# A hybrid decoder on one core: all K pairs of a fast quarter by Winograd, some of their factors made ahead

## The chip, the cores and the metric

The kernel runs on one core of a Trainium2 chip. The time is that of the device in microseconds, from the first to the last instruction and what lies around it; a comparison is between the kernel before and the kernel after on the same chip. The matmul engine is TensorE (PE in the profile), the others are VectorE (DVE), ScalarE (ACT), GpSimd (POOL) and SyncE (SP), which here only issues transfers.

## The reference

Two layers over 256 positions of width 2048, float32 throughout. Each sub-layer is `x <- LN(alpha*x + f(x))` with `alpha = 4 ** 0.25`:

```python
# layer 0: gated convolution, then MLP
bcu = x @ w_in                       # 2048 x 6144
gate_b, gate_c, u = split(bcu, 3)
y = causal_depthwise_conv(gate_c * u, conv_w, width=3)
x = LN(alpha * x + (gate_b * y) @ w_out)
x = LN(alpha * x + square(relu(x @ w1[0])) @ w2[0])     # 2048 -> 8192 -> 2048
# keys and values from a latent of 512, 16 heads, rotary part of 64
# layer 1: latent attention, then MLP
x = LN(alpha * x + attention(x) @ w_o)
x = LN(alpha * x + square(relu(x @ w1[1])) @ w2[1])
```

## The kernel before

**Products.** A float32 operand is split in a high part, which TensorE multiplies at full speed, and the low rest. `split` (L125 to L128) does it: ScalarE casts (L127), VectorE subtracts (L128). A product of 128 output columns is 16 K tiles of a matmul of 512 columns (`high`, L215: high weights by high and low activations side by side) and one of 256 (`low`, L219: low weights by high activations). The down projections use `dot` (L300, L302, L303), three matmuls of 512 columns: high by high, low weights, low activations.

**The stream of weights.** All weights lie in one list, `stream`, in the order of their use. `take` hands the next entry to TensorE's code and first begins the preparations of the entries up to `LOOK = 5` steps ahead. A plain tile of 1024 columns is one step: a load of 512 KB on SP's queue in a pool of raw tiles (`RAW` of them) and a split into a pool of high and low tiles (`WA` of them). A fast pair is three steps, below. The instruction order in each engine's queue comes from a scheduler; each engine then runs its queue in order.

**The MLP.** The hidden width of 8192 is worked in eight quarters `q` (the kernel's word; a quarter is 1024 columns, eight chunks of 128). A quarter has a product part (eight products, each evacuated, Relu and Square taken, split) and a down part, which adds the quarter's share to the output, 256 by 2048. Quarters 1 to 6 are fast (`FAST`): the output is four column blocks of 512 in two groups `g` of two, the positions are two halves of 128, and a pair of K tiles times a pair of column blocks is done by the Winograd form of Strassen's scheme: seven `dot`s (`FACTORS`: the sums "3", "1", "5", "7", "2", "6", "4") in place of eight. It needs derived factors on both sides. On the weight side `prepare` makes T1 and T3 (L162, 1024 columns), T2 (L166) and T4 (L169, 512 columns each) on VectorE from the pair's two raw tiles and splits all: three splits of 1024 and one of 512. On the side of the hidden activations `form` makes S1 to S4 from two chunks (L707 to L710, four VectorE instructions of 128 columns) and splits them.

The seven sums of a group are more than the eight PSUM banks allow for both groups at once. So a group's sums are copied into PSUM (ScalarE, L612), all pairs are added by TensorE, and the sums copied out (ScalarE, L616), or, where a sum began from zero, added to its place by VectorE (L624). Four of the seven are sums that go to several output blocks and are held in `sums`, the others go to the block they belong to (`acc`); `fold` spreads the held ones in quarter 7. In group 1 only three of the four pairs were fast (`MIXED = "sssp"`); the plain pair's 24 matmuls include one that is done as two halves of 256 (`EVEN`). Group 0 had four fast pairs.

**Around it.** `Norm` works on the residual `xres` (16 chunks), and its `prepare` ran for the residual of MLP0 in quarter 7. In MLP1 `turn_residual` transposes the residual and adds it to `acc` (L1027, L1028), two of eight in each of quarters 1 to 4. In attention the output product's chunks (`out_first`) are interleaved with the stages of the last heads (`together`, with the counts `BEHIND`).

## Time and profile before

| | us |
|---|---|
| median of three runs | 1998.59 (1996.66 to 1999.63) |
| profiled execution, first to last instruction | 1994.9 |
| TensorE busy in it | 1987.7 |
| VectorE busy | 1709.4 |
| ScalarE busy | 1354.9 |
| product part of a fast quarter (536.00 to 580.40) | 44.40 |
| down part of it (580.40 to 619.23) | 38.83 |

The profile has no total of its own for its execution, only the span; the median of the runs is 3.7 us longer than that span. In the profile's rows an L number is a line of the kernel. A group's row reads: line, engine, operation, output and inputs by the program's names, their shapes, the count, then busy time and the mean of one in ns, then the idle time of the engine just before them and what ended it. A timeline row reads: start, length, engine, line, operation, with the idle time before it in brackets. A windows row gives the length of a stretch and each engine's busy time and count in it, then the granted clock, the share of the DMA engines and their GB/s.

### The profile page before, as it was taken

The page shows a single profiled execution, that of the slowest core. Times are in us where ns is not written, and L with a number is a line of the kernel's source. Part 1 is how long each engine was busy: PE and PEld are TensorE (multiplying, and loading weights), DVE is VectorE, ACT ScalarE, POOL GpSimd, SP SyncE. Part 2 cuts the span into 40 slices and gives each one's busy share as a digit, 9 for nine tenths or more (in the row PEclk, how much of TensorE's full clock was granted, in tenths as well). Part 3 has the DMA queues.
Part 4 walks back from the last instruction along what each step waited for, and adds up shares of the span by engine and source line. Part 5 has one row for each costly group of instructions (what it writes and reads, how often), then busy time and mean ns, then how long its engine had stood idle before and what let it go on. Part 6 is the DMA issues. An engine that isn't in the chain of part 4 may idle for free.

```text
span 1994.9 us, 30180 instructions
## 1 busy us (share of the span) xinstructions
PE 1987.7 (100%) x11110; PEld 1737.2 (87%) x11110; DVE 1709.4 (86%) x2555; ACT 1354.9 (68%) x2154; POOL 2.3 (0%) x21
## 2 busy tenths in 40 slices
PE   9999999999999999999999999999999999999998
PEld 8888888988888888888889998898888888888886
DVE  8667667797999989989978988777899999999985
ACT  6444445586778778777756755558677787887772
POOL 0000000000000000000000000000000000000000
PEclk9999999999999999999999999999999999999999
DMA  8666666565657466574855543656464656656483
GB/s 318 205 191 187 190 190 190 179 193 157 212 170 251 148 216 221 177 243 147 281 171 159 170 140 123 201 180 195 146 233 155 232 161 220 222 178 233 150 269 130
DMA packets 106853, 385.85 MB, mean 193 GB/s; under 512 B 11857, under 2 KB 12625, under 8 KB 106449
## 3 DMA queue, kind: packets, MB, share of 16 engines
q1 hardware_dynamic: 106560, 383.79, 59.5%
q8 instruction: 87, 1.43, 0.3%
q14 instruction: 62, 0.50, 0.1%
q10 hardware_dynamic: 144, 0.13, 0.0%
HBM read 381.78 MB, written 2.10 MB: 192 GB/s over the span
## 4 chain that ended last, share of the span: by engine, by line
PE 98%; DVE 1%; ACT 1%; issue 0%; DVEq 0%; ACTq 0%
PE ps_u L215 20%; PE ps_l L215 13%; PE ps_u L219 10%; PE ps_l L219 7%; PE ps_f L300 4%; PE ps_f L303 4%; PE ps_f L302 4%; PE ps_r L303 4%; PE ps_r L302 4%; PE ps_r L300 4%; PE ps_d L300 2%; PE ps_d L302 2%; PE ps_d L303 2%; PE ps_w L249 2%; PE ps_w L248 2%; PE ps_w L247 2%
## 5 line engine op out<-in xcount | busy, mean ns | idle before, releaser
L128 DVE TENSOR_TENSOR lo<-raw,hi 128x1024 fp32r<-128x1024 f32 x710 | 861.8, 1220 | 190.6 <-ACT hi L127 119.9
L127 ACT CAST hi<-raw 128x1024 fp32r<-128x1024 f32 x710 | 741.8, 1051 | 247.4 <-PE ps_l L215 98.1
L215 PE MATMUL ps_u<-xhl,hi 128*128 128x512 f32 x1792 | 621.7, 392 | 0.0
L219 PE MATMUL ps_u<-xhl,lo 128*128 128x256 f32 x1792 | 498.2, 279 | 0.0
L215 PEld LDWEIGHTS ps_u<-xhl,hi 128*128 128x128 f32 x1792 | 334.5, 187 | 73.6 <-ACT acc L595 0.2
L219 PEld LDWEIGHTS ps_u<-xhl,lo 128*128 128x128 f32 x1792 | 338.1, 189 | 1.8
L215 PE MATMUL ps_l<-xhl_a,hi 128*128 128x512 f32 x704 | 244.1, 393 | 0.0
L219 PE MATMUL ps_l<-xhl_a,lo 128*128 128x256 f32 x704 | 195.4, 279 | 0.0
L215 PEld LDWEIGHTS ps_l<-xhl_a,hi 128*128 128x128 f32 x704 | 132.1, 188 | 29.9
L219 PEld LDWEIGHTS ps_l<-xhl_a,lo 128*128 128x128 f32 x704 | 131.9, 188 | 0.2
L127 ACT CAST hi_t<-raw_t 128x1024 fp32r<-128x1024 f32 x84 | 88.5, 1054 | 45.8 <-DVE raw_t L162 41.4
L162 DVE TENSOR_TENSOR raw_t<-raw,raw 128x1024 f32<-128x1024 f32 x84 | 102.3, 1218 | 1.8 <-DMA raw<-in_w2f_dram 1.5
L128 DVE TENSOR_TENSOR lo_t<-raw_t,hi_t 128x1024 fp32r<-128x1024 f32 x84 | 102.4, 1219 | 0.2
L718 ACT ACTIVATE fp<-fp 128x256 f32<-128x256 f32 x96 | 40.0, 416 | 63.2 <-DVE fp L356 62.6
L215 PE MATMUL ps_l<-z,hi 128*128 128x512 f32 x240 | 82.4, 391 | 0.0
L300 PE MATMUL ps_d<-hi,h 128*128 128x512 f32 x192 | 75.0, 391 | 0.0
L302 PE MATMUL ps_d<-lo,h 128*128 128x512 f32 x192 | 75.0, 390 | 0.0
L303 PE MATMUL ps_d<-hi,h 128*128 128x512 f32 x192 | 74.8, 389 | 0.0
L249 PE MATMUL ps_w<-xd,hi 128*128 128x258 f32 x256 | 72.7, 284 | 0.0
L248 PE MATMUL ps_w<-xd,lo 128*128 128x258 f32 x256 | 72.3, 282 | 0.0
L247 PE MATMUL ps_w<-xd,hi 128*128 128x258 f32 x256 | 72.3, 282 | 0.0
L215 PE MATMUL ps_l<-oT,hi 128*128 128x512 f32 x208 | 71.3, 391 | 0.0
(296 smaller groups left out, 3963.7 us busy)
## 6 DMA issues: line engine op xcount, KB each, us to landing
raw<-in_w_dram SPq DMA_DIRECT2D x344, 512.0 KB, 4.5
raw<-in_w2f_dram SPq DMA_DIRECT2D x168, 512.0 KB, 3.9
raw<-in_w_in_dram SPq DMA_DIRECT2D x88, 512.0 KB, 4.2
raw<-in_w_out_dram SPq DMA_DIRECT2D x32, 512.0 KB, 3.7
raw<-in_w_o_dram SPq DMA_DIRECT2D x32, 512.0 KB, 4.2
raw<-in_w_kv_dram SPq DMA_DIRECT2D x10, 512.0 KB, 3.7
raw<-in_w_q_dram SPq DMA_DIRECT2D x8, 512.0 KB, 4.0
raw<-in_w_uk_dram SPq DMA_DIRECT2D x8, 512.0 KB, 3.9
```

Source lines behind the costliest of these rows:

```text
L127: nc.scalar.copy(hi, src)
L128: nc.vector.tensor_tensor(lo, src, hi.bitcast(F32), ALU.subtract)
L162: nc.vector.tensor_tensor(t.rearrange(two, a=2), b12.unsqueeze(1).to_broadcast([P, 2, BW]), r1.rearrange(two, a=2), ALU.subtract)
L215: nc.tensor.matmul(ps, w[blk // 8][0][:, blk % 8, :], x, start=first, stop=False)
L219: nc.tensor.matmul(ps[:, :T], w[blk // 8][1][:, blk % 8, :], x[:, :T], start=False, stop=last)
L247: nc.tensor.matmul(ps[:, :W], hi, x[k][:, :W], start=k == 0, stop=False)
L248: nc.tensor.matmul(ps[:, :W], lo, x[k][:, :W], start=False, stop=False)
L249: nc.tensor.matmul(ps[:, :W], hi, x[k][:, W:], start=False, stop=k == NC - 1)
L300: nc.tensor.matmul(ps, x[0], w[0], start=first, stop=False, skip_group_check=onto)
L302: nc.tensor.matmul(ps[:, at], x[0], w[1][:, at], start=False, stop=False, skip_group_check=onto)
L303: nc.tensor.matmul(ps, x[1], w[0], start=False, stop=last, skip_group_check=onto)
L718: nc.scalar.activation(f, f, AF.Relu)
```

## The change

- Group 1 has four fast pairs too; `MIXED` and `EVEN` go. All eight pairs of a fast quarter now take 7 `dot`s.
- For some pairs the derived factors are made ahead and stored in DRAM: two of eight pairs in each fast quarter of layer 0, one of eight in layer 1 (`EARLY`), eighteen in all. `making` loads the pair's two raw tiles on POOL's queue, makes the three differences on VectorE and stores two tiles of 512 KB on POOL's queue. One step of it is taken in each chunk of the convolution from the seventh on, in every third chunk where the output product is added, and for layer 1 in every second stage of the last heads. `issue_after` ties these to instructions already in POOL's and VectorE's queues. For such a pair `prepare` has four loads and only splits.
- The order of groups alternates by quarter (`groups`), and four sums of the second group stay in PSUM into the next quarter (`stay`). Sums are kept and the next begun one at a time as each ends (`turn`, `end`). The sums "3" and "1" (`FRESH`) always begin from zero and are added to their place by VectorE; the others are copied in and out by ScalarE.
- `hidden` puts the two chunks of a pair into one tile, takes Relu and Square over both at once, and `form` makes the four sums with three instructions and splits seven blocks of 128 in one of 896.
- In MLP0 the residual is written to DRAM in quarter 1, after its `Norm.prepare`, and loaded back in quarter 7 (`parked`, `xback`); `sums` takes its place. In MLP1 all eight `turn_residual` run in quarter 1. The order of `fold` is adapted.
- `RAW` goes from 5 to 7 and `WA` from 8 to 9.

```diff
-RAW, WA = 5, 8
+RAW, WA = 7, 9
...
-MIXED = "sssp"
-EVEN = (QC - 1, "22")
+EARLY = {0: ((1, 0), (1, 2)), 1: ((1, 1),)}
+FRESH = ("3","1")
...
+MAKE_FROM = 6
...
+    held_x = [xres]
+    parked = ctx.enter_context(tc.tile_pool(name="parked", bufs=1, space=bass.MemoryType.DRAM)).tile(
+        [P, NC, T], F32, tag="parked", name="parked")
...
+    def groups(q):
+        return (1, 0) if (q - FAST[0]) % 2 == 0 else (0, 1)
...
+    stored = ctx.enter_context(tc.tile_pool(name="stored", bufs=1, space=bass.MemoryType.DRAM))
+    made = {}
+    for l, q in [(l, q) for l in EARLY for q in FAST]:
+        for i, j in EARLY[l]:
+            t = stored.tile([2, P, 1024], F32, tag=f"m{l}_{q}_{i}_{j}", name=f"made{l}_{q}_{i}_{j}")
+            made[l, q, i, j] = (t[0], t[1])
...
-            for j, kind in enumerate(MIXED):
-                out += [(w2f[l, q, 1, j, 0], w2f[l, q, 1, j, 1])] if kind == "s" else \
-                    halves(w2[l, q, 2, j]) + halves(w2[l, q, 3, j])
-            out += [(w2f[l, q, 0, j, 0], w2f[l, q, 0, j, 1]) for j in range(QC // 2)]
+            for i, g in enumerate(groups(q)):
+                for j in range(QC // 2):
+                    out.append((w2f[l, q, g, j, 0], w2f[l, q, g, j, 1]) + made.get((l, q, i, j), ()))
...
+    def making(l):
+        for (k, q, i, j), (to13, to24) in made.items():
+            if k != l:
+                continue
+            name = f"{l}_{q}_{i}_{j}"
+            r1, r2, t = (raws.tile([P, 1024], F32, tag="raw", name=f"{g}{name}") for g in ("m1", "m2", "m3"))
+            with tc.issue_after(state["pool"].ins):
+                for r, src in zip((r1, r2), w2f[l, q, groups(q)[i], j]):
+                    nc.gpsimd.dma_start(r, src)
+            yield
+            b22, (b21, b12) = r1[:, BW:], (r2[:, :BW], r2[:, BW:])
+            two = "p (a c) -> p a c"
+            with tc.issue_after(state["dve"].ins):
+                nc.vector.tensor_tensor(t.rearrange(two, a=2), b12.unsqueeze(1).to_broadcast([P, 2, BW]),
+                                        r1.rearrange(two, a=2), ALU.subtract)
+                nc.vector.tensor_tensor(r1[:, :BW], b22, t[:, :BW], ALU.subtract)
+                nc.vector.tensor_tensor(r1[:, BW:], b21, r1[:, :BW], ALU.subtract)
+            nc.gpsimd.dma_start(to13, t)
+            state["pool"] = nc.gpsimd.dma_start(to24, r1)
...
+        def fourth(src):
+            f = state["fast"].tile([P, 2, BW], F32R, tag="t4", name=f"t4_{i}", bufs=2)
+            split(f[:, 0, :], f[:, 1, :], src)
+            return [f[:, 0, :], f[:, 1, :]]
...
+        if len(stream[i]) == 4:
+            r1, t13 = load_raw(f"{i}_0", stream[i][0]), load_raw(f"{i}_1", stream[i][2])
+            finished(r1, f"{i}_1")
+            yield
+            t24 = load_raw(f"{i}_2", stream[i][3])
+            b21 = raws.tile([P, 1024], F32, tag="raw", name=f"raw{i}_3")[:, :BW]
+            nc.sync.dma_start(b21, stream[i][1][:, :BW])
+            finished(t13, f"{i}_t")
+            yield
+            finished(t24, f"{i}_2")
+            ready[i] = {**named((("11", "22"), ("T1", "T3"), ("T2", "T4"))), "21": fourth(b21)}
+            yield
+            return
+        r1, r2 = (load_raw(f"{i}_{j}", src) for j, src in enumerate(stream[i]))
...
-    def fast_products(ps, x, forms, j, fresh, ready, onto=()):
+    LEFT = ("11", "22", "12", "S1", "S3", "S2", "S4")
+    def fast_products(ps, x, j, fresh, ready, onto=(), then=None):
         b, = take(1)
-        a = {"11": held(x[2 * j], 0), "12": held(x[2 * j + 1], 0), "22": held(x[2 * j + 1], 1)}
-        for i in range(4):
-            a[f"S{i + 1}"] = [forms[:, j, o, i * P:(i + 1) * P] for o in range(2)]
+        a = {n: [x[j // 2][:, j % 2, o, i * P:(i + 1) * P] for o in range(2)] for i, n in enumerate(LEFT)}
         for p, l, r in FACTORS:
             dot(ps[p], b[r], a[l], p in fresh, p in ready, onto=p in onto)
+            if then:
+                then(p)
...
+    def summed(ln, pss, add, m0=0, maker=iter(())):
         for m, ps in enumerate(pss, m0):
+            if m % 3 == 0:
+                next(maker, None)
             add(ps, m)
             ln.count(m)
...
+        if m >= MAKE_FROM:
+            next(before_mlp, None)
...
+        def first_sums(ps, banks, m):
+            g = groups(q)[0]
+            for p in {3: ("3", "1", "5", "7") if q == FAST[0] else (), 4: "2", 5: "6", 6: "4"}.get(m, ()):
+                banks.setdefault(p, busy[m % 4])
+                ps[p] = begun_sum(p, g, f"ps_r{p}", banks[p])
...
+        def new_sum(p):
+            return p in FRESH or (q == FAST[0] and p in OWN)
...
+        def keep(p, g, ps, since):
...
             at = place(p, g)
-            if q == FAST[0] and p in OWN:
+            if p not in FRESH or (since == FAST[0] and p in OWN):
                 nc.scalar.copy(at, ps)
             else:
                 nc.vector.tensor_tensor(at, at, ps, ALU.add)
...
+        def down_pairs(h, ps, banks, spare):
...
+            order = [p for p, _, _ in FACTORS]
+            stay = order[:4] if q < FAST[-1] else []
+            new = {p for p in order if new_sum(p)}
+            after, place_of = {}, {}
+            def begin_next(p, bank):
+                after[p], place_of[p] = begun_sum(p, second, f"ps_f{p}", bank), bank
+            def turn(p):
+                keep(p, first, ps[p], max(q - 1, FAST[0]) if p in order[:4] else q)
+                i = order.index(p) + 1
+                if i < len(order):
+                    begin_next(order[i], banks[p])
+            def end(p):
+                if p not in stay:
+                    keep(p, second, after[p], q)
+            held_on = set(order[:4]) if q > FAST[0] else set()
             for j in range(n):
-                fast_products(then, h, forms, j, set(then) - onto if j == 0 else (), then if j == n - 1 else (), onto)
-            for p, _, _ in FACTORS:
-                (put_back if p in onto or p in new else keep)(p, 0, then[p])
-            return (b3, b1, b5, b7), (b6, b2, b4, b22)
+                if j == n - 1:
+                    begin_next(order[0], spare)
+                fast_products(ps, h, j, new - held_on if j == 0 else (), ps if j == n - 1 else (),
+                              set(ps) - (new - held_on), turn if j == n - 1 else None)
+            for j in range(n):
+                fast_products(after, h, j, new if j == 0 else (), after if j == n - 1 else (),
+                              set(order) - new, end if j == n - 1 else None)
+            if stay:
+                return [banks[order[-1]]] + [place_of[p] for p in order[4:]], {p: after[p] for p in stay}, \
+                    {p: place_of[p] for p in stay}
+            return [banks[order[-1]]] + [place_of[p] for p in order[:3]], {}, {p: place_of[p] for p in order[3:]}
...
+            def form(j, u):
+                a21, a11, a12, s1, s2, s4 = (u[:, i * P:(i + 1) * P] for i in (0, 1, 3, 4, 6, 7))
+                two = u.rearrange("p (i c) -> p i c", c=P)
+                nc.vector.tensor_tensor(s1, a21, u[:, 2 * P:3 * P], ALU.add)
+                nc.vector.tensor_tensor(two[:, 5:7, :], two[:, 0:5:4, :], a11.unsqueeze(1).to_broadcast([P, 2, P]),
+                                        ALU.subtract)
                 nc.vector.tensor_tensor(s4, a12, s2, ALU.subtract)
-                split(forms[:, j, 0, :], forms[:, j, 1, :], sf.rearrange("p i c -> p (i c)"))
+                f = factors[j // 2][:, j % 2]
...
+                if q in FAST:
+                    if m % 2 == 0:
+                        pair.append(fast.tile([P, 8 * P], F32, tag="fp", name="fp"))
+                    u = pair[-1]
+                    evac(ps, u[:, (m % 2) * T:(m % 2 + 1) * T])
+                    if m % 2:
+                        for function in (AF.Relu, AF.Square):
+                            nc.scalar.activation(u[:, :2 * T], u[:, :2 * T], function)
+                        form(m // 2, u)
+                    return
...
-                    if extra and m == 0 and q <= NB:
+                    if extra and q == FAST[0] and m < NB:
                         for t in range(2):
-                            extra(block, q - 1, t, busy[2 + t])
+                            extra(block, m, t, busy[2 + t])
+                    if begin and q == FAST[0]:
+                        begin(range(max(2 * m, 1), 2 * m + 2))
+                        nc.sync.dma_start(parked[:, 2 * m:2 * m + 2, :], held_x[0][:, 2 * m:2 * m + 2, :])
+                    if q == FAST[0] and m == QC - 1:
+                        sums = act.tile([P, 4, 2, BW], F32, tag="xres", name=f"sums{idx}")
...
-                        if begin:
-                            begin(range(max(2 * m, 1), 2 * m + 2))
+                                last_sum(m - QC + 2, t, list(places.values())[2 * (m - QC + 2) + t])
+                if begin and q == NQ - 1:
+                    held_x[0] = act.tile([P, NC, T], F32, tag="xres", name="xback")
+                    for k in range(0, NC, 4):
+                        nc.sync.dma_start(held_x[0][:, k:k + 4, :], parked[:, k:k + 4, :])
...
                 together(s)
+                if s % 2 == 0:
+                    next(before_mlp, None)
...
-    summed(after, out_chunks(), residual)
+    summed(after, out_chunks(), residual, maker=before_mlp)
```

More of the change, by code (lines that the diff above doesn't have):

```diff
@@ L547, in trunk @@
     ln = Norm(0, ALPHA)
+    before_mlp = making(0)
     for m in range(NC):
@@ L719, in hidden @@
                 nc.scalar.activation(f, f, AF.Square)
[L720 to L725 removed]
+                put_split(h[m], f)
             if q == 0:
@@ L773, in mlp @@
             else:
-                busy, free = down_pairs(h, forms, busy, free, begun)
+                busy, sums_in, places = down_pairs(factors, sums_in, places, busy[3])
     def to_wide(block, put, h):
```

122 lines of the change are left out of this document (32 added, 90 removed).

## The prediction

> **What bounds the kernel now.** I read the page's head first: which engine has no idle time, and which ends the span.
>
> ```profile
> span 1994.9 us, 30180 instructions
> ...
> PE 1987.7 (100%) x11110; PEld 1737.2 (87%) x11110; DVE 1709.4 (86%) x2555; ACT 1354.9 (68%) x2154; POOL 2.3 (0%) x21
> ...
> PEclk9999999999999999999999999999999999999999
> ...
> PE 98%; DVE 1%; ACT 1%; issue 0%; DVEq 0%; ACTq 0%
> ```
>
> TensorE works without a gap at the full granted clock and holds 98% of the chain that ended last. VectorE, at 86%, is the next limit. An average says little about a stage, so I asked for the engines' busy time in windows: one fast quarter of layer 0 (products, then down projection), the next product part, the last fast quarter's down part, three pieces of layer 1, the convolution, and attention with the output product behind it.
>
> ```profile
> core 0: us, PE busy (x) PEld busy (x) DVE busy (x) ACT busy (x) POOL busy (x), PEclk, DMA share, GB/s
> 536.00:580.40 44.40, 44.40 (x258) 39.13 (x257) 39.47 (x56) 35.14 (x58) 0.00 (x0) 1.00 0.63 212
> 580.40:619.23 38.83, 38.83 (x174) 32.15 (x173) 38.66 (x46) 31.33 (x46) 0.00 (x0) 1.00 0.58 185
> 619.23:663.60 44.37, 44.37 (x257) 39.10 (x256) 41.66 (x58) 35.59 (x57) 0.00 (x0) 1.00 0.72 236
> 1394.40:1439.83 45.43, 45.43 (x266) 39.74 (x264) 35.43 (x52) 28.88 (x48) 0.00 (x0) 1.00 0.51 151
> 1523.92:1562.74 38.82, 38.82 (x174) 32.16 (x173) 38.62 (x46) 31.74 (x47) 0.00 (x0) 1.00 0.58 186
> 913.30:953.06 39.76, 39.30 (x174) 32.00 (x173) 39.59 (x48) 32.22 (x48) 0.00 (x0) 1.00 0.54 177
> 28.00:273.00 245.00, 245.00 (x1411) 214.90 (x1410) 167.79 (x248) 115.12 (x155) 1.39 (x14) 1.00 0.66 201
> 1204.00:1232.00 28.00, 27.98 (x169) 24.87 (x168) 20.74 (x60) 13.73 (x37) 0.00 (x0) 1.00 0.32 111
> 1232.00:1304.00 72.00, 72.00 (x416) 63.46 (x415) 59.19 (x101) 40.89 (x59) 0.00 (x0) 1.00 0.62 193
> ```
>
> The reader should see two things. A down part lasts 38.83 us, and in it VectorE is as full as TensorE (38.66): the two race. And before the twelve fast quarters VectorE has room: 245.00 - 167.79 = 77 us in the convolution, 7.3 us in 1204 to 1232. The timeline of TensorE gives the pace inside a down part, first and last row of 42 matmuls:
>
> ```profile
> 609.71 0.39 PE L300 MATMUL ps_f<-hi,forms 128*128 128x512 f32 x1
> ...
> 619.00 0.39 PE L303 MATMUL ps_f<-t,h 128*128 128x512 f32 x1
> ```
>
> 41 intervals in 9.29 us are 0.2266 us for a matmul of 512 columns, whatever it multiplies.
>
> **The change part by part.** The down projection of a fast quarter issued seven fast pairs of 21 matmuls and one plain pair of 24, one of those as two halves: 171 x 0.2266 = 38.75, against 38.83 measured. Now eight fast pairs: 168 x 0.2266 = 38.07. So 0.76 less in each of twelve quarters: **-9.1 us**, all on the path, since TensorE is it. The 913.30 row is 0.93 longer than the others; its place in TensorE's timeline is
>
> ```profile
> 937.97 0.50 PE L300 MATMUL ps_f<-t,h 128*128 128x512 f32 x1 [0.46 <-ACT acc L616]
> ```
>
> a bank kept by ScalarE's copy when one group of sums follows another. The change re-orders just that (each sum is turned over as it ends); it may go or come again: 0 to -0.9, I take -0.4 as the middle.
>
> What pays for this is VectorE. Its groups in a whole fast quarter (536.98 to 620.21):
>
> ```profile
> L128 DVE TENSOR_TENSOR lo<-raw,hi 128x1024 fp32r<-128x1024 f32 x32 | 38.9, 1221 | 4.9 <-ACT hi L127 4.6
> L162 DVE TENSOR_TENSOR raw_t<-raw,raw 128x1024 f32<-128x1024 f32 x7 | 8.5, 1219 | 0.0
> L166 DVE TENSOR_TENSOR raw<-raw,raw_t 128x512 f32<-128x512 f32 x7 | 4.8, 688 | 0.1
> L128 DVE TENSOR_TENSOR t<-raw,t 128x512 fp32r<-128x512 f32 x7 | 4.8, 684 | 0.0
> L128 DVE TENSOR_TENSOR forms<-sf,forms 128x512 fp32r<-128x512 f32 x4 | 2.7, 686 | 0.0
> L624 DVE TENSOR_TENSOR acc<-acc,ps_f 128x512 f32<-128x512 f32 x2 | 1.4, 680 | 0.0
> L709 DVE TENSOR_TENSOR sf<-sf,fp 128x128 f32<-128x128 f32 x4 | 1.2, 288 | 0.1
> ```
>
> and the end of a layer 1 down part, VectorE's rows and then the TensorE row that reads the 1557.81 result:
>
> ```profile
> 1525.53 0.42 DVE L356 TENSOR_TENSOR fp<-ps_u,t 128x256 f32<-128x256 f32 x1
> ...
> 1557.81 1.22 DVE L128 TENSOR_TENSOR lo<-raw,hi 128x1024 fp32r<-128x1024 f32 x1
> 1558.94 0.68 DVE L128 TENSOR_TENSOR t<-raw,t 128x512 fp32r<-128x512 f32 x1
> 1559.55 2.35 DVE L128 TENSOR_TENSOR lo<-raw,hi 128x1024 fp32r<-128x1024 f32 x2
> 1561.82 0.68 DVE L624 TENSOR_TENSOR acc<-acc,ps_f 128x512 f32<-128x512 f32 x1
> ```
> ```profile
> 1560.93 0.39 PE L302 MATMUL ps_f<-lo,h 128*128 128x512 f32 x1
> ```
>
> Instructions start 1.13 us apart at 1024 columns and 0.61 at 512; by the same overlap of 0.08, 0.34 at 256 and 0.2 at 128. A pair whose factors are made in place costs 3 splits + the double difference + two single ones + one split of 512 = 4 x 1.13 + 3 x 0.61 = 6.3 us; an early pair, only split, 3 x 1.13 + 0.61 = 4.0; the plain pair cost 2 x 1.13 = 2.3.
>
> Layer 0, per quarter: from 7 x 6.3 + 2.3 = 46.4 to 6 x 6.3 + 2 x 4.0 = 45.8, so -0.6. Forms: from 4 x (4 x 0.2 + 2 x 0.61) = 8.1 to 4 x (0.2 + 0.34 + 0.2 + 1.0 for a split of 896) = 7.0, -1.1. Adds that keep sums: two of 0.61 for three, -0.6. Together -2.3 us of VectorE's work while TensorE loses 0.76: no new stall, 0.
>
> Layer 1, per quarter: 7 x 6.3 + 4.0 = 48.1, +1.7, and -1.7 from forms and adds: level, but not in the down part. There +1.7 comes on top, TensorE's part is 0.76 shorter, both adds (1.2) now stand ahead of the last weights (before, the add at 1561.82 came behind them), and the lighter forms give back about 0.8 as the last forms spill into this part: 2.9 us more ahead of the last weights. The cushion shown is 1560.93 - 1558.95 = 1.9 us, where a 1557.81 start and 1.13 give the end. A ninth weight buffer lets VectorE enter the part up to half a product earlier (a product of 48 matmuls: 44.37 / 8 = 5.55; half is 2.8). So per quarter between 2.9 - 1.9 - 2.8 = -1.8 (no stall) and +1.0; over six quarters 0 to +6. I take **+1.5**, nearer the low end, as VectorE has 2.7 to 4.9 us idle in the product parts to run ahead in.
>
> The keep adds are also on a path of their own: TensorE's next group may begin in a bank only when the add of its former sum is done, and that add stands in VectorE's queue behind up to two 1.13 us splits. A queue started late by the last evacuation (1525.53, 1.6 us into the part) moves all of it; this is the first rival.
>
> Residual of MLP1: eight adds move from four quarters into the first four products of one:
>
> ```profile
> L1028 DVE SCALAR_TENSOR_TENSOR acc<-turned,acc 128x512 f32<-128x512 f32 x8 | 5.1, 682 | 0.9 <-PE turned L1027 0.9
> ```
>
> VectorE idles 45.43 - 35.43 = 10.0 us in that product part, but six more adds share the banks of the products, and each may hold TensorE for up to one of 0.68: 0 to +3 with the 0.9 idle row doubled at most; I take **+0.8**.
>
> Making in advance: eighteen pairs, each 1.13 + 2 x 0.61 = 2.3 us of VectorE, two loads and two stores of 512 KB on POOL's queue. Twelve fall in the convolution and its output product: 2.3 in each chunk of three products (16.7 us), where VectorE idles 77 / 245 x 16.7 = 5.2: nothing. If that cover were gone they would cost 28 us. DMA rises by 2.1 MB in 16.7 us, from 201 to about 327 GB/s, below the 340 and more of the busiest slices of 2.1 us in the quarter 536 to 620; a load of 512 KB lands in 4.2:
>
> ```profile
> GB/s 293 406 400 279 234 367 343 371 357 328 86 90 197 213 0 12 232 117 146 0 0 230 267 88 257 195 267 205 0 113 373 14 0 259 240 68 234 201 222 281
> ```
> ```profile
> raw<-in_w_in_dram SPq DMA_DIRECT2D x88, 512.0 KB, 4.2
> ```
>
> The other six fall at the last heads and in the output product. There TensorE hangs on VectorE:
>
> ```profile
> 1226.70 0.42 DVE L361 TENSOR_TENSOR oT<-po,oT 128x256 fp32r<-128x256 f32 x1 [1.02 <-ACT oT L360]
> 1229.54 0.42 DVE L361 TENSOR_TENSOR oT<-po,oT 128x256 fp32r<-128x256 f32 x1 [2.42 <-ACT oT L360]
> ```
>
> An insertion of 2.3 into idle times of 1.02 to 2.42 exceeds them by 0 to 1.3; three of them: 0 to +4. I take **+1.5**. The three in 1232 to 1304 have 12.8 us idle: 0. The POOL queue holds nothing else that is urgent (2.3 us busy in all).
>
> SP's queue: in layer 0 eight stores of 256 KB and four loads of 512 KB park and fetch the residual in quarters 1 and 7, and each early pair loads 768 KB more than a pair made in place, 1.5 MB a quarter, 40 GB/s over the 185 of a down part. The DMA share there is 0.58: 0. A load that is late would cost up to its 4.2 us.
>
> ScalarE:
>
> ```profile
> L612 ACT COPY ps_r<-acc 128x512 f32<-128x512 f32 x5 | 2.9, 583 | 0.0
> ```
>
> It has 7.5 us idle in a down part, and gives up nine copies of 0.58 a quarter; Relu and Square of a pair of chunks come as one instruction each, so a pair's last form starts some 0.5 later, four fast pairs before TensorE wants it: 0.
>
> Sum: -9.1 - 0.4 + 1.5 + 0.8 + 1.5 = **-5.7 us**. The span of 1994.9 becomes 1989.2. The profiled execution's span lies 3.7 under the median of the runs, 1998.59; that remains: **1992.9**. A measurement of this kernel tells about 0.2%, 4 us, from no change.
>
> A rule that speaks against the change: a load on GpSimd's queue has its descriptors written by GpSimd. The trace of before has none of that size there. The Trainium skill ("SBUF — State Buffer", section "SBUF: two separate sides") warns that such a transfer starves while VectorE runs an instruction in a two-port mode. Its page "VectorE: DVE Perf Modes" (section "Why `tensor_tensor` can't do 2×_2P or 4×") says two-source instructions have no such mode. The row agrees: 1219 ns for 1024 columns is over one ns a column, with no sign of a doubled rate. By the first rule without the second every load would wait on VectorE, the second rival below.
>
> **The rivals.**
> (1) The keep adds and the last weights of layer 1 are late in every quarter. For it: VectorE's idle time in its down part is 0.2 of 38.82, and 937.97 shows a turn of banks that stalled 0.93. Against: the product part's idle time. At 1.0 to 2 us in each of six, 6 to 12 instead of 1.5: 1997 to 2003, the middle 2000.
> (2) Slower: loads on POOL's queue land late, and VectorE, in order, stands at the making. In the convolution 5.2 - 2.3 = 2.9 us per chunk cover that. In attention there are six makings, issued only some two heads ahead, 8 us, for two loads of 4.2 that may run one after the other. It decides from 9.7 / 6 = 1.6 us of lateness each (5.7 back and 4 more): at 3 us, 1992.9 + 18 = 2011. Against: 111 GB/s there, an idle DMA.
> (3) All is hidden: -9.1 to -10: 1989.
> (4) The change does not do what it says, because VectorE sets the quarters: 78 of 83 us busy. Against: TensorE never waited for a weight in them. It would give 1998.
>
> **How the numbers follow.** The forecast (1990.5 to 1994.5) 0.44; (3) 0.18; (1) 0.20, of it 0.13 within 0.2% and 0.07 slower; (2) 0.12, slower; (4) 0.06, of it 0.04 within and 0.02 slower. Faster by over 0.2%: 0.44 + 0.18 = 0.62; within: 0.17; slower: 0.21. The range from 1988 (all hidden and the 0.93 gone) to 2003 (the upper end of rival 1) leaves out most of (2) and the tails.
>
> **What would show it.** Down parts of 38.1 us in layer 0, with TensorE waiting for nothing; in layer 1 38.1 to 39.1, the surplus as TensorE waiting for VectorE's keep add or a `lo` near the end. At the last heads, TensorE's gap before `po` a few us longer in all. Wrong it would be if VectorE waits at the makings for `raw` from POOL, or if the layer 0 quarters stay at 83.2.

## The result, and the profile after

The changed kernel takes 2032.63 us (2030.49 to 2035.87), the kernel before 1998.57: ratio 1.0171, 95% interval 1.0156 to 1.0185. It is slower by 34 us, where 5.7 us less was forecast. The profiled execution's span is 2028.7, 33.8 over that of before.

The head of the page of the changed kernel, then the rows of its part on transfers:

```profile
span 2028.7 us, 30122 instructions
...
PE 1994.1 (98%) x11062; PEld 1735.0 (86%) x11062; DVE 1735.1 (86%) x2509; ACT 1305.0 (64%) x1950; POOL 41.1 (2%) x93
...
PE 86%; DVE 7%; issue 4%; DMA 2%; ACT 2%; POOL 0%; POOLq 0%; DVEq 0%; ACTq 0%; SPq 0%
```
```profile
m<-in_w2f_dram POOLq DMA_DIRECT2D x36, 512.0 KB, 8.1
made<-m POOLq DMA_DIRECT2D x36, 512.0 KB, 3.9
...
raw<-in_w_out_dram SPq DMA_DIRECT2D x32, 512.0 KB, 5.2
```

TensorE no longer holds the chain to its end: 14% of it lies elsewhere, and transfers are in it. Where the time is lost the windows tell. The stages are cut at the first matmul of each: the convolution's products, its output product, MLP0 up to the end of its last fast quarter, attention's output product, and the six fast quarters of MLP1. First before:

```profile
27.88:278.71 250.83, 250.83 (x1444) 219.97 (x1443) 172.32 (x256) 117.44 (x159) 1.39 (x14) 1.00 0.66 202
278.71:361.93 83.22, 83.22 (x482) 73.37 (x481) 63.21 (x103) 44.71 (x61) 0.00 (x0) 1.00 0.62 187
361.93:953.07 591.14, 590.68 (x3151) 510.36 (x3150) 542.23 (x739) 456.04 (x712) 0.00 (x0) 1.00 0.59 193
1232.12:1304.24 72.12, 72.12 (x418) 63.58 (x417) 59.31 (x100) 41.01 (x59) 0.00 (x0) 1.00 0.62 193
1394.56:1897.38 502.82, 502.82 (x2601) 430.06 (x2600) 471.30 (x611) 392.01 (x601) 0.00 (x0) 1.00 0.59 193
```

The same stages of the changed kernel, and below them one down part of layer 0 and one of layer 1:

```profile
28.00:286.97 258.97, 252.69 (x1445) 219.93 (x1443) 183.93 (x275) 111.22 (x155) 19.77 (x48) 1.00 0.73 246
286.97:381.02 94.05, 87.83 (x482) 75.36 (x481) 77.60 (x120) 45.72 (x63) 7.52 (x14) 0.96 0.84 292
381.02:967.07 586.05, 585.98 (x3127) 506.85 (x3126) 528.69 (x684) 434.94 (x610) 0.00 (x0) 1.00 0.66 216
1246.28:1335.63 89.35, 76.84 (x419) 66.95 (x417) 65.75 (x108) 39.38 (x57) 7.52 (x14) 0.92 0.79 282
1425.94:1931.08 505.14, 502.76 (x2578) 426.11 (x2577) 471.40 (x570) 367.66 (x497) 0.00 (x0) 1.00 0.61 201
598.89:637.01 38.12, 38.12 (x171) 31.53 (x169) 34.53 (x40) 30.72 (x42) 0.00 (x0) 1.00 0.67 213
1640.63:1680.36 39.73, 39.00 (x170) 31.19 (x169) 37.78 (x45) 29.08 (x40) 0.00 (x0) 1.00 0.60 180
```

| stage | before | after | difference |
|---|---|---|---|
| convolution | 250.83 | 258.97 | +8.1 |
| its output product | 83.22 | 94.05 | +10.8 |
| MLP0 to the end of quarter 6 | 591.14 | 586.05 | -5.1 |
| attention's output product | 72.12 | 89.35 | +17.2 |
| quarters 1 to 6 of MLP1 | 502.82 | 505.14 | +2.3 |

They sum to +33.3 of the 33.8. The three stages with makings lose 36.1 us; the quarters, which were to gain, gain 5.1 in layer 0 (as forecast) and lose 2.3 in layer 1.

In the steady part of the convolution a chunk takes 18.06 us in place of 16.7 (three products of 5.55), and each chunk has one halt of TensorE. Two of them, from TensorE's timeline, then what ScalarE and VectorE do around the first, and POOL:

```profile
211.03 0.50 PE L267 MATMUL ps_l<-xhl_a,hi 128*128 128x512 f32 x1 [1.10 <-ACT hi L161]
229.08 0.50 PE L267 MATMUL ps_l<-xhl_a,hi 128*128 128x512 f32 x1 [1.10 <-ACT hi L161]
```
```profile
209.66 0.37 ACT L409 COPY t<-ps_l 128x256 f32<-128x256 f32 x1 [5.18 <-PE ps_l L271]
209.93 1.05 ACT L161 CAST hi<-raw 128x1024 fp32r<-128x1024 f32 x1
```
```profile
214.75 1.22 DVE L128 TENSOR_TENSOR m<-m,m 128x1024 f32<-128x1024 f32 x1
...
220.24 0.68 DVE L131 TENSOR_TENSOR m<-m,m 128x512 f32<-128x512 f32 x1
```
```profile
204.37 1.20 POOL L123 DMA_DIRECT2D m<-in_w2f_dram  x2 [0.56 <-issue]
...
221.32 0.54 POOL L133 DMA_DIRECT2D made<-m  x1 [4.41 <-DVE cbuf L410]
```

The reader should see how long a making keeps its tiles: loads at 204.37, VectorE's turn from 214.75 to 220.92, between its other work, the second store issued at 221.32, landed 6.4 later. So the tile that is stored last is held for 23 us, more than a chunk. A making's three tiles are three of the seven raw tiles that the weight loads use in turn: a chunk takes six for weights and three for a making, nine, so within the same chunk the loads come round to tiles that a making still holds. SP's own waits say it, from 182 to 262 us:

```profile
SPq L172 <- DMA made<-m: 39.3, 7, 8.8
SPq L172 <- DVE lo L162: 19.3, 9, 3.9
```

SP stands 39.3 of 80 us for the makings' stores. But at these halts no weight is late. The load that the cast at 209.93 reads was issued at 201.16 (its row, alone in the window 201.1 to 201.3), so it had landed 5 us before the cast:

```profile
raw<-in_w_in_dram SPq DMA_DIRECT2D x1, 512.0 KB, 3.7
```

What holds the cast is its place in ScalarE's queue: right behind an evacuation that itself waits for TensorE (209.66, 5.18 idle). TensorE waits for a cast that waits for TensorE, once a chunk, at 18.06 us. The other four such halts, from 192.97 to 265.20, read the same.

In attention's output product VectorE is what stands. It waits for the makings' loads, 15.8 us in four waits from 1246 to 1336, and behind a making stand the adds that ScalarE waits for and the splits of the weights:

```profile
DVE m L128 <- DMA m<-in_w2f_dram: 15.8, 4, 7.3
```
```profile
1263.92 1.22 DVE L128 TENSOR_TENSOR m<-m,m 128x1024 f32<-128x1024 f32 x1 [6.20 <-DMA m<-in_w2f_dram]
...
1276.77 1.23 DVE L128 TENSOR_TENSOR m<-m,m 128x1024 f32<-128x1024 f32 x1 [7.26 <-DMA m<-in_w2f_dram]
```
```profile
1266.50 0.42 ACT L478 ACTIVATE sq<-xback 128x256 f32<-128x256 f32 x1 [9.29 <-DVE xback L555]
```
```profile
1268.30 0.80 PE L267 MATMUL ps_l<-oT,hi 128*128 128x512 f32 x1 [8.80 <-ACT hi L161]
1279.19 0.58 PE L271 MATMUL ps_l<-oT,lo 128*128 128x256 f32 x1 [3.70 <-DVE lo L162]
```

The cast of the 1268.30 halt starts at 1267.22, behind that `sq`; the tile it reads had landed at 1261.99.

Theory A1 is that tiles held by a making, met in rotation by the weight loads, are the cause. Its rivals: the landing of loads on POOL's queue (A2), VectorE's 2.3 us a making (A3), or something else in the change altogether (B).

### The profile page after: what moved, and what is told of

It reads as the page before. It is cut to its first block, busy times and chain, and to the rows that moved or that the text cites. A ratio compares the mean times of both kernels' runs of the same rounds, so it can differ in the third digit from the quotient of the medians.

```text
span 2028.7 us, 30122 instructions
## 1 busy us (share of the span) xinstructions
PE 1994.1 (98%) x11062; PEld 1735.0 (86%) x11062; DVE 1735.1 (86%) x2509; ACT 1305.0 (64%) x1950; POOL 41.1 (2%) x93
## 4 chain that ended last, share of the span: by engine, by line
PE 86%; DVE 7%; issue 4%; DMA 2%; ACT 2%; POOL 0%; POOLq 0%; DVEq 0%; ACTq 0%; SPq 0%
PE ps_u L267 19%; PE ps_l L267 11%; PE ps_u L271 10%; PE ps_l L271 6%; PE ps_f L354 5%; PE ps_f L355 5%; PE ps_f L352 5%; DVE lo L162 2%; PE ps_d L352 2%; PE ps_d L355 2%; PE ps_d L354 2%; PE ps_r L354 2%; PE ps_r L355 2%; PE ps_r L352 2%; DMA m<-in_w2f_dram 2%
## 5 line engine op out<-in xcount | busy, mean ns | idle before, releaser
L161 ACT CAST hi<-raw 128x1024 fp32r<-128x1024 f32 x710 | 733.6, 1052 | 234.8 <-PE ps_u L267 77.1
L161 ACT CAST hi_t<-raw_t 128x1024 fp32r<-128x1024 f32 x78 | 82.1, 1052 | 60.1 <-DVE raw_t L218 45.5
L218 DVE TENSOR_TENSOR raw_t<-raw,raw 128x1024 f32<-128x1024 f32 x78 | 95.0, 1218 | 11.0 <-DMA raw<-in_w2f_dram 10.1
L162 DVE TENSOR_TENSOR lo_t<-raw_t,hi_t 128x1024 fp32r<-128x1024 f32 x78 | 95.0, 1218 | 3.6 <-ACT hi_t L161 3.4
L409 ACT COPY t<-ps_l 128x256 f32<-128x256 f32 x44 | 16.4, 372 | 112.4 <-PE ps_l L271 112.4
L161 ACT CAST t<-raw 128x512 fp32r<-128x512 f32 x96 | 59.7, 622 | 23.3 <-DVE raw L225 9.9
```

Source lines behind the costliest of these rows:

```text
L161: nc.scalar.copy(hi, src)
L162: nc.vector.tensor_tensor(lo, src, hi.bitcast(F32), ALU.subtract)
L218: nc.vector.tensor_tensor(t.rearrange(two, a=2), b12.unsqueeze(1).to_broadcast([P, 2, BW]), r1.rearrange(two, a=2), ALU.subtract)
L409: nc.scalar.copy(t, ps[:, T:])
```

## The experiments

Medians are of kernels run beside the kernel before; ratios are to it, with the 95% interval.

### No making at all

```diff
-EARLY = {0: ((1, 0), (1, 2)), 1: ((1, 1),)}
+EARLY = {}
```

> The changed kernel without making in advance: no pair's factors are stored, every pair of a fast quarter makes its own in place; all else is as changed. The traces put the change's loss in the convolution and its output product (+19.1 us from 27.9 us to the start of MLP0) and in the attention's output product (+17.2). Theory A (the makings cost all of it): both fall to about 0, so the span comes to 2028.7 - 36 = about 1992 to 1998; the layer 0 quarters may lose up to 1 us each as VectorE gets 4.6 us more per quarter. Rival B (the loss is in the other edits of the change, the re-ordered sums or the buffers): the time stays above 2015.

2017.82 us, ratio 1.0096 (1.0079 to 1.0113). The number lies in B's range, and yet neither expectation held as a whole. The stages with makings are clean: 250.8 for the convolution, 83.2 for its output product, 73.5 for attention's, so A is right on their 36 us; 1.4 of the last are there without a making. But the quarters lose what was to be spared:

```profile
362.35:961.71 599.36, 594.64 (x3119) 504.23 (x3117) 553.11 (x714) 429.35 (x602) 0.00 (x0) 1.00 0.59 193
1407.26:1915.88 508.62, 506.82 (x2570) 423.55 (x2568) 482.88 (x586) 365.73 (x492) 0.00 (x0) 1.00 0.57 189
```

599.36 for MLP0 where the changed kernel has 586.05, so 13.3 us more, and 508.62 for 505.14. (In this run the first matmul of the next product part stands ahead of the last of the down part, which end 3.2 us later in both layers; with them the losses are up to 16.5 and 6.7.) Eight pairs in place in every quarter are too much for VectorE. The makings are needed: without them the saved matmuls are a loss.

### A pool of its own for layer 0's makings

The pool is closed again before MLP0's own pool is opened, in whose place it lies.

```diff
-            r1, r2, t = (raws.tile([P, 1024], F32, tag="raw", name=f"{g}{name}") for g in ("m1", "m2", "m3"))
+            r1, r2, t = (state.get("mk", raws).tile([P, 1024], F32, tag="raw", name=f"{g}{name}") for g in ("m1", "m2", "m3"))
...
-    before_mlp = making(0)
+    before_mlp, mk_stack = making(0), ExitStack()
+    state["mk"] = mk_stack.enter_context(tc.tile_pool(name="mk0", bufs=3))
...
+    mk_stack.close()
+    del state["mk"]
```

> The changed kernel, but layer 0's makings take their three tiles from a pool of their own, open only during the convolution and its output product, in place of three of the seven raw tiles that SP's weight loads use in turn. Theory A1 (the makings hold tiles that the weight loads come round to, and SP's queue stands until the stores of a making have landed): the 19.1 us of the convolution stage fall to 0 to 5, the span to about 2010 to 2015. Rival A2 (loads on POOL's queue land late, 8.1 us, and VectorE stands) and rival A3 (VectorE's 2.3 us per making are the cost): the stage stays at +15 or more, the span above 2024.

2012.19 us, ratio 1.0066 (1.0051 to 1.0081): 20.4 us back. The convolution, its output product, and attention's output product, where nothing was changed:

```profile
28.16:279.00 250.84, 250.84 (x1445) 219.97 (x1444) 192.06 (x283) 118.19 (x160) 20.33 (x49) 1.00 0.81 276
279.00:362.21 83.21, 83.21 (x482) 73.36 (x481) 69.20 (x114) 41.93 (x61) 6.99 (x13) 1.00 0.81 269
1227.79:1317.39 89.60, 76.59 (x419) 66.40 (x417) 64.18 (x106) 38.06 (x56) 7.51 (x14) 0.92 0.80 281
```

Both stages are as before the change to 0.01 us, with all twelve makings in them, the same VectorE work, the same transfers on POOL's queue (still 7.7 us to landing), and a higher rate (276 GB/s). SP no longer waits for a `made` (182 to 262 us):

```profile
SPq L172 <- DVE lo L162: 49.5, 20, 3.9
SPq L172 <- DVE cbuf L410: 26.4, 10, 2.7
```

For these stages A2 and A3 fall as costs in themselves, and A1 holds in this: the loss is there only when the tiles are shared. Its path is not the one that I had in mind. ScalarE's queue has another order in this kernel, cast and evacuation by turns as before the change, where the changed kernel has two evacuations in a row ahead of the casts:

```profile
219.58 0.37 ACT L409 COPY t<-ps_l 128x256 f32<-128x256 f32 x1 [1.55 <-PE ps_l L271]
219.84 1.05 ACT L161 CAST hi<-raw 128x1024 fp32r<-128x1024 f32 x1
222.54 1.06 ACT L161 CAST hi<-raw 128x1024 fp32r<-128x1024 f32 x1 [1.64 <-PE ps_l L267]
```

That the scheduler set the casts back because it reckoned with loads that wait for the makings' tiles is argued, not shown. Nor is it shown that the tiles must be apart: the kernel has ten now in place of seven, and ten in one pool was not run.

### The makings' loads on SP's queue

```diff
-                    nc.gpsimd.dma_start(r, src)
+                    nc.sync.dma_start(r, src)
```

> The changed kernel with the two loads of each making on SP's queue in place of POOL's; the stores stay on POOL's. Rival A2 (POOL's queue is the cause: its descriptors or its late issue): at least 15 of the 36 us come back, the time at 2018 or less. Theory A1 (tiles shared in rotation): 2025 to 2045, as the same tiles are held as long.

2007.74 us, ratio 1.0045 (1.0029 to 1.0061), 25 us back: A1 as I stated it missed, and the number is in A2's range. The stages are 256.68, 86.67 and 73.40. The loads land in 4.5 us in place of 8.1, though the tiles are still shared. In the convolution and its output product 9.3 of the 19 us remain. In attention's output product all but the 1.3 that is there without a making comes back, with the tiles shared as before: VectorE no longer waits for a making's load there (2.0 us in all, for a store, in place of 15.8). So in attention the late landing was the cost, A2, as far as this run and the waits tell; tiles of their own were not tried there. In the convolution it is a cost only with shared tiles, as the last experiment, below, tells. On POOL the loads are issued right behind the previous making's stores, 1 MB; that this is why they take 8.1 is argued, not shown.

### The makings without VectorE's work

```diff
-            with tc.issue_after(state["dve"].ins):
-                nc.vector.tensor_tensor(t.rearrange(two, a=2), b12.unsqueeze(1).to_broadcast([P, 2, BW]),
-                                        r1.rearrange(two, a=2), ALU.subtract)
-                nc.vector.tensor_tensor(r1[:, :BW], b22, t[:, :BW], ALU.subtract)
-                nc.vector.tensor_tensor(r1[:, BW:], b21, r1[:, :BW], ALU.subtract)
-            nc.gpsimd.dma_start(to13, t)
+            nc.gpsimd.dma_start(to13, r2)
```

> The changed kernel with the three VectorE subtractions of each making left out; the raw tiles are stored in their place, so the derived factors of those pairs are wrong. All transfers and tiles stay. Rival A3 (VectorE's 2.3 us and its waits in order are the cost): the 36 us vanish, about 1995. Theory A1: part of it, as a tile is given back as soon as its load and store have landed, no longer after VectorE's turn one chunk later: 2005 to 2025.

1996.17 us, ratio 0.9989 (0.9979 to 0.9999), all 36 us back, A3's number; the stages are 250.83, 83.22 and 73.47. But VectorE's time itself was not the cost, since the run with a pool of its own kept it and lost nothing in the convolution. What goes with the subtractions is the waiting: VectorE never stands for a making's load, the loads land in 5.1 us, and the second store is issued 7 to 9 us after the first load in the convolution, in place of 17. So the tiles come free sooner too, and this run can't tell the two apart. The third tile of a making is never written in it.

### All eighteen makings in the convolution

The kernel with the pool of its own, with one list of makings for both layers, begun in the fourth chunk; none in attention.

```diff
-MAKE_FROM = 6
+MAKE_FROM = 3
...
-    before_mlp = making(1)
...
-                if s % 2 == 0:
-                    next(before_mlp, None)
```

> The kernel with a pool of its own for the makings, and now all eighteen in the convolution and its output product (from the fourth chunk on), none in the attention. Theory A1 (the makings' tiles in the rotation of the weight loads are the whole cost): the attention's output product, +17.5 in the run before, falls to +1.5 (that much it has without any making), so the span goes from 2011.1 to about 1994 to 1996, the time to 1996 to 1999, the same as before the change within 0.2%. Rival (the transfers' volume is the cost as well: DMA share 0.90 from 200 to 273 us with twelve): with eighteen the convolution stalls by 5 us or more, the time 2001 or more.

1995.82 us, ratio 0.9984 (0.9975 to 0.9993): the lowest median of all, 0.16% under the kernel before. The interval leaves out 1, but the difference is less than the 0.2% that the prediction gave for what a measurement can tell. Attention's output product takes 73.50, the convolution with its output product 250.83 and 83.18, at a DMA share of 0.87 and 301 GB/s. So the volume of transfers costs nothing here, and the change's loss, but for attention's 1.4, was in where the makings took their tiles and where they were put.

```profile
27.99:278.82 250.83, 250.83 (x1446) 220.09 (x1445) 197.94 (x291) 118.95 (x161) 26.23 (x60) 1.00 0.87 301
1391.25:1897.04 505.79, 503.69 (x2578) 426.52 (x2576) 471.25 (x570) 367.17 (x497) 0.00 (x0) 1.00 0.60 200
```

What is left is layer 1: its quarters take 505.79, more than the 502.82 before.

### Two early pairs in layer 1 too

```diff
-EARLY = {0: ((1, 0), (1, 2)), 1: ((1, 1),)}
+EARLY = {0: ((1, 0), (1, 2)), 1: ((1, 0), (1, 2))}
...
-        for i, j in EARLY[l]:
+        for i, j in EARLY[l][:1 if (l, q) == (1, 1) else 2]:
...
-MAKE_FROM = 3
+MAKE_FROM = 0
...
-            if m % 3 == 0:
+            if m % 2 == 0:
                 next(maker, None)
```

> As conv18, with two early pairs in each layer 1 quarter but the first: 23 makings, one in every chunk of the convolution and one in every second chunk of its output product. Theory B1 (layer 1's stalls, 38.2 to 39.7 us a down part against 38.1, are VectorE's work on the factors of a seventh pair in place): these quarters become like those of layer 0, 38.1 and 44.4, and another 4 to 6 us come back: 1991 to 1995. Rival B2 (they are the re-ordered sums: the keep adds on VectorE and the copies): layer 1 stays as in conv18. If the transfers saturate (23 makings at 126 GB/s beside 190 to 245), the convolution stalls by 5 us or more, and the time is above 2000.

2013.87 us, ratio 1.0074 (1.0061 to 1.0087). Layer 1 does what B1 says: every down part 38.1, every product part after the first 44.4, the six quarters 499.64, 6.2 less than in the run with 18. But the density in the output product is too high:

```profile
282.31:371.42 89.11, 84.30 (x482) 74.19 (x481) 61.86 (x101) 33.09 (x48) 14.49 (x27) 0.98 0.78 286
371.42:523.06 151.64, 138.88 (x838) 125.07 (x837) 126.22 (x209) 99.05 (x159) 3.23 (x6) 0.93 0.68 218
1416.31:1915.95 499.64, 499.18 (x2578) 427.65 (x2577) 458.65 (x555) 368.83 (x498) 0.00 (x0) 1.00 0.64 211
```

5.9 lost there, 16.4 at MLP0's start, where TensorE waits for splits, and 2.9 ahead of the convolution's products, which begin at 31.5 in place of 28.6. So B1 is shown, and a limit to how dense makings may stand. What sets it is again VectorE at a making whose load is late, now with tiles of its own. From 282 to 390 us it waits 22.2 us in five such waits; behind the one below stand the splits that TensorE waits 10.15 us for.

```profile
379.70 1.23 DVE L126 TENSOR_TENSOR m<-m,m 128x1024 f32<-128x1024 f32 x1 [4.74 <-DMA m<-in_w2f_dram]
```

### No sum kept by VectorE

```diff
-FRESH = ("3","1")
+FRESH = ()
```

(on the kernel with 18 makings in the convolution)

> As conv18, but no sum is kept by VectorE: "3" and "1" are copied in and out of PSUM by ScalarE as the others. Theory B1 (factors): layer 1's down parts shorten or stay within 0.5 us each, as VectorE loses two adds of 0.6 a quarter: -3 to +1 us in all. Rival B2 (the keep adds stand in VectorE's queue ahead of the last weights, the prediction's first rival): the stalls of 39.7 go, -3 to -6 us. If ScalarE's copies in turn hold the banks, as the 0.93 us of the kernel before did, it is slower by 1 to 10 us.

2003.76 us, ratio 1.0025 (1.0016 to 1.0034), 8 us slower than with them. The quarters of layer 1 take 510.63 for 505.79 (and another 1.6 to the last matmul of the last down part), though VectorE has less to do. This is the third outcome that was expected, in which ScalarE's copies cost more than the adds, so alone it does not clear the adds. B2, the prediction's first rival, falls by the run before: with both adds in place a second early pair took the stalls away.

### Eight weight buffers

```diff
-RAW, WA = 7, 9
+RAW, WA = 7, 8
```

(on the kernel with 18 makings in the convolution)

> As conv18 with eight weight buffers in place of nine. The prediction gave the ninth up to 2.8 us of cushion in a down part of layer 1. If so, layer 1's down parts lose 0.5 to 2.8 us more each, +3 to +15 us in all; if VectorE never gets so far ahead that the ninth is used, nothing changes (within 2 us).

2006.6 us, ratio 1.004 (1.0026 to 1.0054), 10.8 slower. The quarters of layer 1 take 512.34 for 505.79, and another 1.9 to the last matmul of the last down part: 1.1 to 1.4 each. The ninth buffer is worth that; it was put at up to 2.8.

### 21 and 20 makings

A second early pair in quarters 1, 3 and 5 of layer 1 (21), or in 3 and 5 (20), begun in the first or second chunk, and every third chunk in the output product as with 18.

```diff
-EARLY = {0: ((1, 0), (1, 2)), 1: ((1, 1),)}
+EARLY = {0: ((1, 0), (1, 2)), 1: ((1, 0), (1, 2))}
...
-        for i, j in EARLY[l]:
+        for i, j in EARLY[l] if l == 0 or q in (1, 3, 5) else ((1, 1),):
```

> As conv18 with a second early pair in quarters 1, 3 and 5 of layer 1: 21 makings, from the first chunk of the convolution on, in its output product one in every third chunk as in conv18. Theory B1 (layer 1's stalls are VectorE's work on a seventh pair): the stalls of quarters 3 and 5 (39.8 for 38.1 and 45.3 for 44.4, 2.6 us each) and the 0.5 of quarter 1 go: about 5.5 us under conv18, 1990 to 1991. If the loss of the run with 23 came from the density of makings in the output product, nothing stalls here; if it came from their number, the stage before MLP0 stalls by 5 us or more and the time is 1996 or more.

> As conv18 with a second early pair in quarters 3 and 5 of layer 1 alone: 20 makings, from the second chunk on. Theory B1: 2.6 us of each of the two quarters come back, about 5 us under conv18, 1990.5 to 1992, and the other quarters of layer 1 stay at 38.2 to 38.6. If the stalls of quarters 3 and 5 came from their order of groups and not from the weights' work, they stay: 1995 to 1997.

1995.97 (ratio 0.9989, 0.9980 to 0.9998) and 1997.37 (0.9992, 0.9983 to 1.0001): as with 18, where 4 to 6 us less were expected of both. The convolution does not stall (250.8 and 83.2 in both), so it was the density. The stalls of quarters 3 and 5 went, 38.4 and 44.4 each, but quarters 4 and 6, with one early pair, now take 1.3 to 1.6 us more than 38.12 and 44.39, part of it in the product part behind quarter 6: a stall had let VectorE catch up, and without it the shortness is carried on. The start also loses about 1 us: the convolution's products begin at 29.8 in place of 28.6. With 21, one down part of layer 0 takes 39.1.

### 21 makings, spread over both layers

```diff
-        for i, j in EARLY[l]:
+        for i, j in EARLY[l] if (l, q) not in ((0, 3), (0, 6), (1, 6)) else ((1, 1),):
```

> 21 makings as in conv21, but spread evenly over the two layers: two early pairs in every fast quarter but the third and sixth of layer 0 and the sixth of layer 1, which have one. Theory B1 (a quarter with two has VectorE's work to spare, one with a single pair is about 0.8 us short, and what is short is carried to the next): layer 0 stays within 1 us of 38.1 and 44.4 a quarter, layer 1 falls to 38.1 and 44.4 but for its last, so 4 to 5 us under conv18, 1990.5 to 1992.5. If the shortness of one quarter costs its whole 1.6 to 2.6 us each time, 1993 to 1996.

1997.04 us, ratio 0.9994 (0.9983 to 1.0005), a miss by 5. Layer 1 came out as expected, 38.1 and 44.4 but for the last. But layer 0 gave up 3.9 us up to attention's output product, and the products begin 1.8 us later: all that was gained. A quarter with one early pair costs 1.3 to 1.5 us here, in either layer.

### 18 makings with loads on SP's queue

```diff
-                    nc.gpsimd.dma_start(r, src)
+                    nc.sync.dma_start(r, src)
```

(on the kernel with 18 makings in the convolution)

> As conv18, the two loads of each making on SP's queue. If the long landing on POOL's queue (8.4 us against 4.5 on SP's) is a cost in itself, this is faster than conv18 by 2 us or more. If it only mattered because the weight loads shared the tiles, it is within 2 us of conv18's 1995.8; if SP's queue, now holding loads that wait for the making's own tiles, delays the weights behind them, it is slower by 3 us or more.

1996.57 us, ratio 0.9994 (0.9985 to 1.0003), the same as with POOL's queue (1995.82). With tiles of their own, and at this density, the makings' loads may land in 8.4 us or in 6.5: it costs nothing, though VectorE waits 13.0 us for them in the convolution and its output product with POOL's queue. So what SP's queue gave back there in the first kernel was not its own price. In attention no making stands in this run.

## Why the prediction was wrong

- **The saving, -9.1 and -0.4.** Right where the weights keep up: 38.12 in every down part of layer 0 against 38.07 forecast, and in all of layer 1 with 23 makings. That is 0.71 less than before in place of 0.76. The 0.93 stall went as well, all of it: -5.1 in MLP0 for -4.6 and -0.4.
- **Layer 0, VectorE lighter: 0.** Right.
- **Layer 1, 0 to +6, taken +1.5.** It measured +5.1, within the bounds and 3.6 over what was taken. The down parts of the changed kernel take 232.8 in all, 4.1 more than six of 38.12, and product parts after a stall another 1.0. The mechanism was the stated one, VectorE's work on a seventh pair in place: a second early pair removes it. What I had not seen is that such a stall is carried from quarter to quarter.
- **The residual in one quarter, +0.8.** Of the right size: that product part takes 49.29; the four of before, 45.27 each from their first matmul, are 0.88 over a plain one of 44.39, all of which in one part would make 47.9, so +1.4.
- **The making in advance: 0 in the convolution, +1.5 in attention.** This is the step that failed: it measured 36.1 (8.1 + 10.8 + 17.2), of which 1.4 are not the makings'. I costed what a making does, VectorE's 2.3 us against 5.2 idle and 126 GB/s against what the busiest slices moved. Both were indeed free in the convolution with own tiles. I put at nothing what a making holds: three of the seven tiles of the weight loads, the last of them 17 us to the issue of its store and 6.4 more to its landing. The change shows both, the tiles taken from `raws` and the larger `RAW`; neither was worked out. That was 19 of the 36 us. At the halts it came by way of the order of ScalarE's and VectorE's queues, not of late weights. And I took VectorE's idle time, 12.8 us from 1232 to 1304, for cover. But VectorE works in order: standing for loads it left TensorE without casts and splits, and attention's output product lost 17.2.
- **Rival 2**, loads on POOL land late and VectorE stands at the making, is what happened in attention: four waits of 15.8 us in all, where 2011 was reckoned from 3 us each. For the convolution its cover, 2.9 us of VectorE's idle time a chunk, did hold: VectorE's waits for loads were not what stopped TensorE there (in its output product one halt, 1.41 us at 302.51, came so). It did not see the shared tiles.
- **The Trainium skill's rule** ("SBUF — State Buffer", "SBUF: two separate sides") on starved transfers of GpSimd's queue spoke for the right side: loads there took 8.1 us against 4.5 on SP's queue. Whether starved descriptors are the reason no run here shows; they took 5.1 us when the makings' subtractions were left out.
- **Rival 1**, the keep adds, fell: with them in place and a second early pair the stalls of layer 1 are gone (499.64 for 505.79). **Rival 4** was half right: VectorE does set the quarters as soon as all eight pairs are made in place (599.36 and more for 591.14).

What stays open: why attention's output product takes 73.4 to 73.5 with nine weight buffers even where nothing stalls it, 1.4 over before (with eight it is 72.1); why the scheduler orders ScalarE's queue otherwise when the tiles are shared; and whether three more tiles in the shared pool would have done.

## What to carry to other kernels

When work is moved ahead, cost what it holds and for how long, beside what it does: count the allocations of the shared pool over one period (here nine in a ring of seven), and if the holder's release lies a period or more away, whatever shares the ring waits for it in order. A few buffers of its own, alive only in that stage, made the same work free, up to a density. Before a halt is put down to a late load, look up when that load landed: here the order of a queue was what bound. Idle time of an engine that works in order is no cover for work that must wait for a load. And where one engine is a little short in each period, a stall in one period hides the shortness of the next: look at the sum over periods, not at the stall.

## What the runs showed of the hardware

After a halt TensorE's granted clock is lower for some time. In attention's output product of the changed kernel it idles 12.5 us (8.80 + 3.70), and the rows around it are

```profile
1260.00:1280.00 20.00, 8.00 (x34) 6.65 (x35) 8.61 (x12) 4.79 (x6) 2.67 (x5) 0.78 0.63 232
1280.00:1300.00 20.00, 20.00 (x103) 17.50 (x102) 15.88 (x23) 8.58 (x11) 2.15 (x4) 0.87 0.92 330
```

In the second, without any wait, only 103 matmuls ran in 20 us, where the stage's rate before is 116 (418 in 72.12). The stage lost 17.2: 12.5 idle, the 1.4 it has anyway, and some 3.3 that are left for the slow pace.

After a short halt the pace can be lower too, at a granted clock of 1.00. In the kernel with 18 makings quarter 3's down part has a stall of two waits; the product part behind it is 0.9 longer than one without, at the same count:

```profile
1561.38:1605.76 44.38, 44.38 (x257) 39.15 (x256) 41.18 (x51) 32.33 (x45) 0.00 (x0) 1.00 0.68 237
1605.76:1645.54 39.78, 39.04 (x171) 31.21 (x169) 37.82 (x45) 29.11 (x40) 0.00 (x0) 1.00 0.58 181
1645.54:1690.84 45.30, 45.30 (x257) 39.19 (x256) 42.70 (x54) 33.73 (x46) 0.00 (x0) 1.00 0.66 231
```

Each pair of matmuls there takes 0.353 us, not 0.347, evenly over the whole part, and the next down part runs at its full pace. So a stall of 1.6 cost 2.6. It is not always so: in the changed kernel the same stall of quarter 3 (the 1640.63 row of the result) is followed by a part of 44.51. Why the pace stays, and that the halt is its cause, is not shown.
